# VectorE's order in the top-k zone of a two-layer decoder trunk, and one transfer moved in its second mixer

## The chip, the cores and the metric

One core of one Trainium2 chip (trn2). The metric is the device time of one execution in microseconds, the median of the runs. One more execution was recorded by the profiler; all rows below come from that one.

## What is computed

The reference is a decoder trunk of two layers over 256 tokens of width 1024, all in float32. Cut to what matters here:

```python
for l in range(2):
    h = x @ w_in[l] + b_in[l]                       # one projection, split into the groups' inputs
    y_lru = _rg_lru(...)                            # convolution, gates, linear recurrence
    y_nsa = _nsa(...)                               # attention: compressed, selected, window
    mix = concat([rms(y_lru), rms(y_nsa)]) @ w_out[l]
    x = layer_norm(ALPHA * x + mix)
    x = layer_norm(ALPHA * x + _peer(x, ...))

def _peer(x, wq, subkeys, u_tab, v_tab):            # 16384 experts, 8 heads, 16 chosen per head
    q = (x @ wq).reshape(T, 8, 2, 128)
    s = einsum('thcd,ckd->thck', q, subkeys)        # scores against 2 x 128 keys
    sv, si = top_k(s, 16)
    cv, ci = top_k(all 16 x 16 sums of the two halves, 16)
    experts, gate = ..., softmax(cv)
    act = gelu(x . u_tab[experts]);  y = (act * gate) . v_tab[experts]
```

The gates of the recurrence are two sigmoids of small block-diagonal matmuls (`lru_wa`, `lru_wx`).

## The kernel before, in words

One program runs everything on one core. A layer has two parts.

**The mixer.** Its steps (projections, convolution, recurrence, attention, output projection, norms) are named by short codes, and a string per layer, `ORDER[l]` (L29 to L38), sets the order in which they are issued; the loop that reads it is at L715. `d0` to `d5` are transfers of constants (`const_load`, L666), issued on SyncE's queue: `d0` the table `cmix`, `d1` the gate weights `lw` (512 KB, L670), `d2` and `d3` the halves of `cw1` (512 KB each, L672), `d4` `cw2` (L674), `d5` the residual in the first layer only. `V0` to `V3` are the convolutions on VectorE (L361, L364), `G0` to `G3` the gates of the recurrence, which read `xc` and `lw` on TensorE (L370); `g`, `c`, `q`, `k` are projections (`proj`, L322). In the second layer the buffers of the mixer are those that the stage before it used, so its constants can be loaded only when that stage's last matmuls have read them.

**The experts.** No gather is done: all 16384 experts' activations are computed densely, as 128 tiles of 128 experts (`u_tile`, L739). A tile is loaded (512 KB), split into a high and a low part, and multiplied in three passes. The split is `wtile` (L96): ScalarE casts the high part `hi` (L103), and POOL (for the first 14 tiles, `NPOOL`) or VectorE (for the rest) subtracts to get the low part `lo` (L104); TensorE then runs 24 matmuls (`col_mm`, L114), of which the third is the first to need `lo`. There are four buffers for the raw tile and three each for `hi` and `lo`. Queries 4 to 7 of the experts' heads are made by the same routine, two tiles each, split on VectorE (`query`, L768).

Beside the u-tiles runs the **top-k zone** (L750 to L920), list work on VectorE. `top(h)` (L791) takes the scores of head h (eight matmuls on TensorE, L798, a copy `ss` by ScalarE, L800) and finds the 16 best of 128 keys in four pieces, each a chain of five steps (`best16`, L784: maximum, index, replace, maximum, index). `pairs(g)` (L808) forms 50 candidate sums for eight lists (L812, L816) and finds their 16 best in eight pieces. `choices(g)` (L830) turns indices into experts by wide comparisons and sums (L834 to L874), and `turn_round` (L878) transposes the result on TensorE and copies it. `work()` (L892) strings these together as a generator; each piece yields what it is reckoned to cost on VectorE, and the loop at L914 keeps an account: a piece's cost is taken off `room`, and whenever `room` is negative the next u-tile is issued, which adds 2.88 (a POOL tile) or 1.66 (a VectorE tile). A query adds 2 x 2.88 and takes 2 x 1.22. By that account the program's order in the middle of the zone is: the last pieces of `pairs(0)`, both tiles of query 4, both of query 5, four pieces of `top(4)`, query 6, `top(5)`, u-tile 12, query 7, `top(6)`, u-tile 13, two pieces of `top(7)`, u-tile 14, one piece, u-tile 15, one piece, u-tile 16, then `pairs(1)`, `choices(0)`, `choices(1)`, with a u-tile after every 1.7 us or so of list work.

This is the order in which instructions are written down. A scheduler then orders each engine's instructions when the program is compiled; it may put an instruction of later in the program ahead of one that is not ready by its own reckoning. The next stage (L961) makes one-hot matrices and goes on with the u-tiles that are left, 124 in all before its end.

Of the kernel before, what the change touches and what calls it, by code (L numbers as in the profile page):

```python
# [20 lines left out]
D = 1024  # L21
S = 256
# [27 lines left out]
NPOOL = 14  # L50
# [27 lines left out]
def trunk_kernel(ctx: ExitStack, tc: tile.TileContext, x, xt, cst, lam, pvec, brow, w_in, w_lx, w_v, w_q4, lru_w,  # L78
# [13 lines left out]
    def bank():  # L92
        return psp.tile([128, 512], F32, tag="ps", name="ps")


    def wtile(src, shape, lo_eng, dst=None):  # L96
        n = int(np.prod(shape))
        raw = ring.tile([128, 1024], F32, tag="raw", name="raw", bufs=4)
        if dst is None:
            dst = (ring.tile([128, 1024], F32R, tag="hi", name="hi"), ring.tile([128, 1024], F32R, tag="lo", name="lo"))  # L100
        nc.sync.dma_start(raw[:, :n], src)
        hi, lo, raw = dst[0][:, :n], dst[1][:, :n], raw[:, :n]
        ACT.copy(hi, raw)  # L103
        lo_eng.tensor_tensor(lo, raw, hi, op=ALU.subtract)  # L104
        if len(shape) == 2:
            hi = hi.rearrange("p (a b) -> p a b", a=shape[0])
            lo = lo.rearrange("p (a b) -> p a b", a=shape[0])
        return hi, lo
# [5 lines left out]
    def col_mm(ps, w, xT, t=ALL):  # L114
        for c in range(NCH):
            mm3(ps, (w[0][:, c, :], w[1][:, c, :]), (xT[0][:, c, t], xT[1][:, c, t]), c == 0, c == NCH - 1)
# [149 lines left out]
    for l in range(NL):  # L266
# [461 lines left out]
        with tc.tile_pool(name="peer", bufs=1, reuse_waits="tile") as pp:  # L728
# [7 lines left out]
            def act_tile():  # L736
                return pp.tile([128, 2, S], F32, name="act", bufs=NACT)

            def u_tile(a):  # L739
                if a % 2 == 0:  # L740
                    ub[a] = bank()
                ps = ub[a - a % 2]
                col_mm(ps[:, HALF[a % 2]], wtile(u_tab[l, a], (8, 128), POOL if a < NPOOL else DVE), xT)
                if a % 2:
                    at = act_tile()
                    ACT.activation(at.rearrange("p a b -> p (a b)"), ps, AF.Gelu_apprx_tanh)  # L746
                    kept[a - 1] = spill.tile([128, 2, S], F32, name="kept%d" % (a - 1), bufs=1)
                    ACT.dma_start(kept[a - 1], at)

            with tc.tile_pool(name="topk", bufs=1, reuse_waits="tile") as tk:  # L750
# [17 lines left out]
                def query(h):  # L768
                    qh = tk.tile([128, 2, S], F32, name="qh", bufs=2)
                    if h < 2:  # L770
                        for tb in range(2):
                            ACT.copy(qh[:, :, TB[tb]], qT4[tb][:, 2 * h:2 * h + 2])
                    else:
                        ps = bank()
                        for c in range(2):
                            k = 2 * h + c - 4
                            if "w%d" % k in W:
                                raw_mm(ps[:, c * 256:c * 256 + 256], W["w%d" % k])
                            else:
                                col_mm(ps[:, c * 256:c * 256 + 256], wtile(wq[l, k], (8, 128), POOL if h < 4 else DVE), xT)  # L780
                        ACT.copy(qh.rearrange("p a b -> p (a b)"), ps)
                    qhs[h] = qh
# [8 lines left out]
                def top(h):  # L791

                    qh = qhs.pop(h)
                    ps = bank()
                    for tb in range(2):
                        for c in range(2):
                            k = tb * 2 + c
                            PE.matmul(ps[:, k * 128:k * 128 + 128], qh[:, c, TB[tb]], skt[:, c], start=True, stop=True)  # L798
                    ss = tk.tile([128, 4, 128], F32, name="ss", bufs=2)
                    ACT.copy(ss.rearrange("p a b -> p (a b)"), ps)  # L800
                    s2 = tk.tile([128, 4, 128], F32, name="s2", bufs=2)
                    for tb in range(2):
                        for c in range(2):
                            k, j = tb * 2 + c, tb * 4 + h % 4
                            best16(sv[:, h // 4, j, c], si[:, h // 4, j, c], ss[:, k], s2[:, k])
                            yield 1.45

                def pairs(g):  # L808

                    a, b = sv[:, g, :, 0], sv[:, g, :, 1]  # L810
                    for i in range(8):
                        DVE.tensor_tensor(cd[:, :, OFF[i]:OFF[i] + CNT[i]], a[:, :, i:i + 1].to_broadcast([128, 8, CNT[i]]),  # L812
                                          b[:, :, :CNT[i]], op=ALU.add)
                        if i % 4 == 3:
                            yield 1.2
                    DVE.tensor_tensor(cd[:, :, OFF[8]:NCAND], a[:, :, 8:16],  # L816
                                      b[:, :, 0:1].to_broadcast([128, 8, 8]), op=ALU.add)
                    for j in range(8):
                        best16(cv[:, g, j], ci[:, g, j], cd[:, j], c2[:, j])
                        yield 1.05  # L820
# [57 lines left out]
                def turn_round():  # L878
                    for w in range(3):
                        ps = bank()  # L880
                        for tb in range(2):
                            src = ev[:, w, tb] if w < 2 else gate[:, tb]
                            PE.transpose(ps[:, TB[tb]], src.rearrange("p g k -> p (g k)"), ident)
                        tok = ps[:, :256].rearrange("p (q i) -> p q i", i=2)
                        if w < 2:
                            DVE.tensor_copy(eT[:, :, w], tok)
                        else:
                            DVE.tensor_scalar(gT[:, :, 0], tok, GSC, None, op0=ALU.mult)
                            DVE.scalar_tensor_tensor(gT[:, :, 1], tok, GSC, gT[:, :, 0], op0=ALU.mult, op1=ALU.subtract)
                        yield 0.5  # L890

                def work():  # L892
                    for h in (2, 0, 1, 3):
                        yield from top(h)
                    yield from pairs(0)
                    query(4)
                    yield 2.44 - 5.76
                    for h in range(4, 8):
                        if h < 7:
                            query(h + 1)  # L900
                            yield 2.44 - 5.76
                        yield from top(h)
                    yield from pairs(1)
                    yield from choices(0)
                    yield from choices(1)
                    yield 1.0
                    yield from turn_round()
                    yield 4.0
# [3 lines left out]
                        q_rows(1)  # L912
                    query(h)
                a, room = 0, 0.0  # L914
                for cost in work():
                    room -= cost
                    while room < 0 and a < 96:
                        u_tile(a)
                        room += 2.88 if a < NPOOL else 1.66
                        a += 1  # L920

            with tc.tile_pool(name="dense", bufs=1, reuse_waits="tile") as dp:

# [356 lines left out]
```

## Time and profile before

| what | value |
|---|---|
| runs, median (lowest to highest) | 1939.76 us (1935.61 to 1939.79), 3 runs |
| the profiled execution, its own time | 1938.31 us |
| its span | 1936.5 us |
| busy: TensorE, VectorE, ScalarE, POOL | 98%, 69%, 50%, 4% |
| share of the chain that ended last: TensorE, VectorE, DMA | 88%, 8%, 2% |

Times are microseconds from the start of the span. A busy share is an average over the whole span; the top-k zones lie at about 160 to 300 us (first layer) and 1120 to 1270 us (second layer), the start of the second mixer at about 987 us. PEclk is the clock that TensorE was granted, as a share of 2.4 GHz. Matmuls are pipelined, so a tile's own time is best read from the chain of waits, where pieces don't overlap.

### The profile page before, as it was taken

Reading aid. Unit: us, or ns where it says so; the run is one execution under the profiler, and the core shown is the slowest. Engines: PE = TensorE matmul, PEld = TensorE weight load, DVE = VectorE, ACT = ScalarE, POOL = GpSimd, SP = SyncE. Lnnn points to the kernel's source line nnn. Section 1 sums busy time; section 2 is a strip of 40 time slices with the busy share of each in tenths; the row PEclk is TensorE's granted clock in tenths of the full one; section 3 lists DMA queues with packets and bytes.
Section 4 is the critical chain, followed back from the end, with each engine's and each line's share of the span. In section 5 each row is a group of like instructions: output and inputs, shape, how many; then the busy total and the mean of one; then the engine's idle time right before and its main releaser. Section 6 shows DMA issues by size and latency. Waiting matters only on the chain.

```text
span 1936.5 us, 32461 instructions
## 1 busy us (share of the span) xinstructions
PE 1894.0 (98%) x12580; PEld 1679.2 (87%) x12580; DVE 1330.6 (69%) x2553; ACT 966.3 (50%) x1579; POOL 83.1 (4%) x55
## 2 busy tenths in 40 slices
PE   8999899999999999999999998999999999999998
PEld 7858899999999888888777498999999998888886
DVE  5763994766666776767657549946666656777776
ACT  3635444555555555556445344444555555555553
POOL 0005200000000000000000062000000000000000
PEclk9999999999999999999999999999999999999999
DMA  7505557666667777888362054576666677778783
GB/s 267 175 1 172 153 191 236 211 207 192 204 203 242 244 241 240 282 283 300 140 227 66 0 187 154 189 236 212 196 203 201 201 245 240 244 243 286 250 265 106
DMA packets 130095, 393.91 MB, mean 203 GB/s; under 512 B 15634, under 2 KB 16404, under 8 KB 129812
## 3 DMA queue, kind: packets, MB, share of 16 engines
q1 hardware_dynamic: 111508, 358.28, 57.8%
q10 hardware_dynamic: 18432, 33.56, 4.7%
q8 instruction: 98, 1.61, 0.3%
q14 instruction: 57, 0.47, 0.1%
HBM read 357.18 MB, written 34.60 MB: 202 GB/s over the span
## 4 chain that ended last, share of the span: by engine, by line
PE 88%; DVE 8%; DMA 2%; issue 1%; ACT 1%; SPq 0%; POOL 0%; DVEq 0%; ACTq 0%; POOLq 0%
PE ps L112 39%; PE ps L995 34%; PE ps L954 3%; PE ps L119 3%; PE ps L590 3%; DVE lo L104 1%; PE ps L562 1%; DMA raw<-in_v_tab_dram 1%; PE ps L515 1%; DVE si L789 1%; DVE cd L812 1%; PE ps L232 1%; DVE s L787 1%; DVE si L786 0%; DVE t L866 0%
## 5 line engine op out<-in xcount | busy, mean ns | idle before, releaser
L104 DVE TENSOR_TENSOR lo<-raw,hi 128x1024 fp32r<-128x1024 f32 x516 | 635.1, 1232 | 396.4 <-ACT hi L103 396.0
L103 ACT CAST hi<-raw 128x1024 fp32r<-128x1024 f32 x548 | 575.1, 1050 | 663.4 <-PE ps L112 412.0
L112 PE MATMUL ps<-xThi,lo 128*128 128x256 f32 x2400 | 685.4, 286 | 20.0 <-DVE lo L104 19.7
L112 PE MATMUL ps<-xThi,hi 128*128 128x256 f32 x2400 | 693.5, 289 | 0.0
L112 PE MATMUL ps<-xTlo,hi 128*128 128x256 f32 x2400 | 684.0, 285 | 0.0
L995 PE MATMUL ps<-hi,W 128*128 128x512 f32 x1936 | 517.8, 389 | 0.0
L112 PEld LDWEIGHTS ps<-xThi,lo 128*128 128x128 f32 x2400 | 465.4, 194 | 21.9 <-DVE lo L104 21.2
L112 PEld LDWEIGHTS ps<-xThi,hi 128*128 128x128 f32 x2400 | 465.7, 194 | 0.9 <-issue 0.4
L112 PEld LDWEIGHTS ps<-xTlo,hi 128*128 128x128 f32 x2400 | 465.8, 194 | 0.3
L995 PEld LDWEIGHTS ps<-hi,W 128*128 128x128 f32 x1936 | 363.2, 188 | 75.4
L995 PE MATMUL ps<-lo,W 128*128 128x512 f32 x968 | 298.1, 389 | 0.2 <-DVE lo L104 0.2
L995 PEld LDWEIGHTS ps<-lo,W 128*128 128x128 f32 x968 | 181.6, 188 | 38.2 <-DVE lo L104 0.6
L986 ACT CAST W<-act 128x256 fp32r<-128x256 f32 x242 | 96.1, 402 | 94.6 <-PE ps L995 90.4
L987 DVE TENSOR_TENSOR W<-act,W 128x256 fp32r<-128x256 f32 x242 | 100.0, 422 | 9.5
L104 POOL TENSOR_TENSOR lo<-raw,hi 128x1024 fp32r<-128x1024 f32 x32 | 79.6, 2493 | 355.9 <-ACT hi L103 355.6
L972 DVE TENSOR_TENSOR act<-act,G 128x512 f32<-128x512 f32 x128 | 87.5, 685 | 6.6 <-DMA act<-kept 6.6
L958 ACT ACTIVATE G<-ps 128x256 f32<-128x256 f32 x256 | 81.2, 383 | 5.3
L943 DVE TENSOR_TENSOR ohg<-ohg,gT 128x2048 f16<-128x2048 f16 x64 | 78.2, 1225 | 2.0
L939 DVE TENSOR_TENSOR ohg<-iota,eT 128x2048 f16<-128x2048 f16 x64 | 77.9, 1220 | 0.0
L746 ACT ACTIVATE act<-ps 128x512 f32<-128x512 f32 x128 | 75.7, 591 | 0.1
L954 PE MATMUL ps<-ohg 128*128 128x128 f16 x1024 | 69.9, 219 | 0.0
L954 PEld LDWEIGHTS <-ohg 128*128 128x128 f16 x1024 | 58.8, 97 | 2.8
(256 smaller groups left out, 1179.6 us busy)
## 6 DMA issues: line engine op xcount, KB each, us to landing
raw<-in_u_tab_dram SPq DMA_DIRECT2D x256, 512.0 KB, 3.6
raw<-in_v_tab_dram SPq DMA_DIRECT2D x256, 512.0 KB, 4.2
kept<-act ACTq DMA_DIRECT2D x128, 256.0 KB, 2.5
act<-kept SPq DMA_DIRECT2D x128, 256.0 KB, 4.1
raw<-in_w_in_dram SPq DMA_DIRECT2D x24, 512.0 KB, 4.5
raw<-in_wq_dram SPq DMA_DIRECT2D x24, 512.0 KB, 3.6
ow<-in_w_out_dram SPq DMA_DIRECT2D x16, 512.0 KB, 7.8
qf<-in_w_q_dram SPq DMA_DIRECT2D x8, 512.0 KB, 3.8
```

The source lines that it names most:

```text
L103: ACT.copy(hi, raw)
L104: lo_eng.tensor_tensor(lo, raw, hi, op=ALU.subtract)
L112: PE.matmul(ps, a[m], b[n], start=start and i == 0, stop=stop and i == 2)
L746: ACT.activation(at.rearrange("p a b -> p (a b)"), ps, AF.Gelu_apprx_tanh)
L939: DVE.tensor_tensor(oh.rearrange("p q w a i -> p (q w) a i"), iota.unsqueeze(1).to_broadcast([128, 8, 128, 2]), eT[:, qs].rearrange("p q w ...
L943: DVE.tensor_tensor(og, oh[:, :, 0:1].to_broadcast([128, 4, 2, 128, 2]), gT[:, qs].unsqueeze(3).to_broadcast([128, 4, 2, 128, 2]), op=ALU. ...
L954: PE.matmul(ps[:, k * 128:k * 128 + 128], oh[:, q, 1, :, i], og[:, q, w, :, i], start=w == 0, stop=w == 1)
L958: ACT.activation(G[g][:, :, t1:t1 + 4], ps.rearrange("p (t g a) -> p g a t", g=2, a=64)[:, g], AF.Copy, scale=1.0 / GSC)
L972: i = DVE.tensor_tensor(act[a0], act[a0], G[a0 // 64][:, a0 % 64:a0 % 64 + 2, :], op=ALU.mult)
L986: ACT.copy(whi, at[:, a % 2])
L987: DVE.tensor_tensor(wlo, at[:, a % 2], whi, op=ALU.subtract)
L995: PE.matmul(accs[tb * 2 + hf], ww[m][:, TB[tb]], v[n][:, hf * 512:hf * 512 + 512], start=a == first[0] and (m, n) == (0, 0), stop=a == 127 ...
```

## The change

It has three edits. In the second layer's order, `d1` moves from behind `V3` to directly behind `d0`. The loop that issues the top-k zone stands in a block that keeps VectorE's instructions in the order in which they are written; the other engines are ordered as before. And a VectorE u-tile adds 1.6 to `room` instead of 1.66, so that 48 instead of 47 u-tiles are issued within the zone.

```diff
-         "c0 I1 I0 d0 d4 P c1 V0 d2 V2 V1 d3 V3 d1 G0 d5 G3 G1 T g1 b0 g0 b1 g2 h0 g3 G2 q2 h1 D S q3 q1 kv q0 "
+         "c0 I1 I0 d0 d1 d4 P c1 V0 d2 V2 V1 d3 V3 G0 d5 G3 G1 T g1 b0 g0 b1 g2 h0 g3 G2 q2 h1 D S q3 q1 kv q0 "
...
                 a, room = 0, 0.0
-                for cost in work():
-                    room -= cost
-                    while room < 0 and a < 96:
-                        u_tile(a)
-                        room += 2.88 if a < NPOOL else 1.66
-                        a += 1
+                with tc.manual_schedule(engines={mybir.EngineType.DVE}):
+                    for cost in work():
+                        room -= cost
+                        while room < 0 and a < 96:
+                            u_tile(a)
+                            room += 2.88 if a < NPOOL else 1.6
+                            a += 1
```

## Rows read from the trace of the kernel before

**Rows 1.** The page, busy time of each engine over the span.
```profile
PE 1894.0 (98%) x12580; PEld 1679.2 (87%) x12580; DVE 1330.6 (69%) x2553; ACT 966.3 (50%) x1579; POOL 83.1 (4%) x55
```
**Rows 2.** Busy time by stretch: stretch, length, busy us, PEclk, DMA share, GB/s.
```profile
205.00:215.00 10.00, 7.28 (x49) 7.07 (x49) 9.97 (x58) 5.35 (x7) 0.00 (x0) 0.83 0.33 109
231.00:245.00 14.00, 11.81 (x87) 11.61 (x86) 14.00 (x67) 4.64 (x7) 3.54 (x1) 0.88 0.33 114
256.00:266.00 10.00, 6.03 (x38) 5.82 (x38) 10.00 (x59) 1.47 (x2) 0.00 (x0) 0.83 0.47 165
...
1170.00:1180.00 10.00, 6.12 (x49) 5.71 (x48) 9.97 (x45) 4.97 (x6) 0.00 (x0) 1.00 0.31 91
1196.00:1208.00 12.00, 9.83 (x71) 9.63 (x70) 12.00 (x56) 2.70 (x3) 3.49 (x1) 0.86 0.39 133
1220.00:1235.00 15.00, 11.03 (x70) 10.82 (x69) 14.15 (x85) 3.63 (x4) 0.00 (x0) 0.77 0.60 191
```
**Rows 3.** Waits of TensorE, 155 to 300 and 1118 to 1286: us, times, longest.
```profile
PE ps L112 <- DVE lo L104: 8.9, 3, 4.0
...
PE ps L112 <- DVE lo L104: 10.0, 4, 4.0
```
**Rows 4.** Timeline of VectorE, 128-wide pieces: start us, duration us, instruction.
```profile
175.82 0.28 DVE L787 MATCH_REPLACE8 s<-sv,ss 128x128 f32<-128x128 f32 x1
176.14 0.30 DVE L788 MAX8 sv<-s 128x8 f32<-128x128 f32 x1
176.47 0.09 DVE L789 MATCH_VALUE_LOAD si<-sv,s 128x8 f32 x1
...
256.26 0.31 DVE L785 MAX8 sv<-ss 128x8 f32<-128x128 f32 x1
256.46 0.30 DVE L788 MAX8 sv<-s 128x8 f32<-128x128 f32 x1
...
257.43 0.31 DVE L785 MAX8 sv<-ss 128x8 f32<-128x128 f32 x1
```
**Rows 5.** Timeline of VectorE, additions, 50-wide pieces and splits.
```profile
200.30 2.88 DVE L812 TENSOR_TENSOR cd<-sv 128x128 f32<-128x128 f32 x6
...
206.27 0.20 DVE L785 MAX8 cv<-cd 128x8 f32<-128x50 f32 x1
...
207.06 0.21 DVE L785 MAX8 cv<-cd 128x8 f32<-128x50 f32 x1
...
209.42 1.22 DVE L104 TENSOR_TENSOR lo<-raw,hi 128x1024 fp32r<-128x1024 f32 x1
...
211.51 2.29 DVE L851 TENSOR_TENSOR ge<-cif,i 128x2048 f16<-128x2048 f16 x1
...
259.35 0.73 DVE L812 TENSOR_TENSOR cd<-sv 128x128 f32<-128x128 f32 x6
```
**Rows 6.** Timeline of ScalarE: copies of query 5 and of top4's scores.
```profile
224.52 0.58 ACT L781 COPY qh<-ps 128x512 f32<-128x512 f32 x1
225.00 0.59 ACT L800 COPY ss<-ps 128x512 f32<-128x512 f32 x1
```
**Rows 7.** TensorE: two tiles in the chain of waits; the matmuls of one top.
```profile
186.69 5.75 PE ps L112 x48
...
185.63 1.06 PE L798 MATMUL ps<-skt,qh 128*128 128x128 f32 x8
```
**Rows 8.** Timelines at the second mixer's start: SyncE's queue, VectorE, TensorE.
```profile
987.90 0.48 SPq L674 DMA_DIRECT2D cw<-in_cmp_w_dram  x1
...
990.39 0.54 SPq L670 DMA_DIRECT2D lw<-in_lru_w_dram  x1
...
995.27 0.48 DVE L364 SCALAR_TENSOR_TENSOR xc<-xpad,pvec_sb,xc 128x256 f32<-128x256 f32 x1
...
996.87 2.36 DVE L104 TENSOR_TENSOR lo<-raw,hi 128x1024 fp32r<-128x1024 f32 x2
...
997.39 2.83 PE L370 MATMUL ps<-xc,lw 128*128 128x256 f32 x12 [3.15 <-DMA lw<-in_lru_w_dram]
```

## The prediction

> **What bounds the kernel now.** I read the busy shares first: TensorE works 98% of the span [rows 1], so a change pays only where TensorE waits or runs at the lower of its two clock levels. Busy time cut into stretches shows where that is inside the top-k zones (155 to 300 us in the first layer, 1118 to 1286 us in the second): in six stretches [rows 2]. TensorE's idle time there is 2.72, 2.19 and 3.97 us in the first layer, 8.9 in all, and 3.88, 2.17 and 3.97 in the second, 10.0 in all. The granted clock falls in five of the six. Stretch times missing clock share gives 1.7 + 1.7 + 1.7 = 5.1 us in the first layer and 0 + 1.7 + 3.4 = 5.1 in the second: behind a short wait TensorE runs a while at 1.2 instead of 2.4 GHz. All that this zone can give back is thus 8.9 + 5.1 + 10.0 + 5.1 = 29 us. The list of waits names who ends them: VectorE's splits (`lo`, L104), and nothing else of any weight [rows 3]. VectorE is busy through nearly all six stretches, so each wait is a matter of order: list work stood in front of a split that TensorE wanted.
>
> VectorE's order now is not that of the program. `choices(0)` is written behind `pairs(1)`, yet its line L851 runs at 211.5 us, among the splits of queries 4 and 5 [rows 5]. And list instructions of two pieces are interleaved: the first maximum of one piece runs beside the second of the one before [rows 4].
>
> **The change, part by part.**
>
> *Program order, price of a piece.* `best16` is a chain: maximum, index, replace, maximum, index. Where neighbours are independent, a 128-wide maximum is followed after 0.20 us; where the next needs its result, after 0.33 (176.14 to 176.47), and behind a replace 0.32 (175.82 to 176.14) [rows 4]. A piece has three such joints. Interleaved, a 128-wide piece takes 1.17 us (256.26 to 257.43) and a 50-wide one 0.79 (206.27 to 207.06) [rows 4, 5]. In program order I add 3 x 0.125 = 0.37: 1.54 and 1.16. With three joints at 0.125 the lower bound is 0 (all hidden by a neighbour), the upper 0.4; I take nearly the upper, since program order puts the dependent ones side by side. The plan in `work()` reckons with 1.45 and 1.05, so it is some 0.1 us short per piece.
>
> [...]
>
> *Query 4's first split.* It stands behind all of `pairs(0)` in the program. The nine additions end at 203.18 us, held up now (2.88 us for six, 0.73 in the second group) [rows 5]; top(3)'s own joints, 4 x 0.37, lie partly in that hold. Eight pieces at 1.16 then end at 212.5. The split, now at 209.42 between two pieces, starts some 3.5 us later (3 to 4.6). The tiles before it are split on POOL and end where they do, so this wait grows from 2.7 to some 6.2, less what TensorE waits now for the query's second split, which will follow at once: 5.5. Bounds 2.7 and 6.7.
>
> *Queries 6 and 7, and u-tile 14.* The order in the program is Q4 Q5 top4 Q6 top5 u12 Q7 top6 u13, half of top7, u14, each Q being two tiles whose splits are VectorE's; u12 and u13 are split on POOL. Now VectorE fills the time with `choices(0)`; pinned, it cannot. It must wait for top4's scores, which TensorE computes behind Q5's tiles: the copy of query 5 is at 224.52, that of top4's scores at 225.00 [rows 6]. Only then come four pieces (4 x 1.54 = 6.2), then Q6's first split. A tile is 5.75 / 2 = 2.88 us on TensorE, the scores' matmuls about 0.8 to 1.06 [rows 7]. So:
> - before Q6: 0.7 (copy of the scores) + 6.2 + 1.2 (a split, [rows 5]) = 8.1 us without a split; TensorE has u12 (2.9) if it is put forward, and two matmuls (0.2): 5.0 idle.
> - before Q7: 1.1 (Q6's second split, overlapped) + 6.2 + 1.2 = 8.5, against two tiles and two matmuls, 6.0: 2.5 idle.
> - before u14: 1.1 + 6.2 + 3.1 + 1.2 = 11.6, against two tiles, u13, scores and two matmuls, 9.7: 1.9 idle.
>
> Bounds: nothing for each if the scores are computed early; and 7.9, 5.0 and 8.1 if TensorE, too, keeps strict program order, where each top's scores come behind the next query's tiles (0.7 + 6.2 + 1.2 - 0.2 without u12; the same less u12; the same with half of top7, 3.1, less u13). I take the sums above, because in the trace a ready instruction is put into a gap.
>
> *After u14.* A tile's share is 1.6 us of list plus 1.14 of split (two take 2.36, one 1.22 [rows 5, 8]), under 2.88: no wait, and the third stretch of each layer loses its reason. `room` 1.66 to 1.6 puts one more u-tile into the zone and one less into the next stage, whose number is the same in sum: 0. `turn_round` copies now wait in VectorE's queue for transposes that stand behind tiles on TensorE; a split behind them comes late by at least itself, 1.2, less two matmuls, 0.2: 1.0 once per layer. ACT's exponential and casts lie beside this work.
>
> *Clock.* Five falls cost 10.2 us, 2.0 each (1.7 to 3.4). For four or five waits per layer I take 3.5 falls: 7.1 instead of 5.1, 2.0 more per layer.
>
> Zone: waits 5.5 + 5.0 + 2.5 + 1.9 + 1.0 = 15.9. First layer 15.9 - 8.9 + 2.0 = +9.0, second 15.9 - 10.0 + 2.0 = +7.9.
>
> *Gate weights first (second mixer).* `d1` moves from the last to the second place of the five transfers on SyncE's queue, ahead of `d4`, `d2`, `d3`. TensorE waits 3.15 us for `lw`, until 997.39; its issue was at 990.39 and moves to about 987.9, where `d4` is now [rows 8], 2.5 us earlier, with about 1.1 MB less in front of it. The wait goes, but the next is near: the third convolution chain ends at 995.75, and the next projection's split, at 996.87, is done by 998.1, against 1000.2 now (997.39 + 2.83, where its work gets TensorE): 2.1 us gained, bounds 0 and 3.15. `d2` and `d3` come 0.5 MB later; they are needed later, at the first hidden layer, behind two more projections. The first mixer's order is unchanged.
>
> Sum: 9.0 + 7.9 - 2.1 = +14.8 on the profiled execution's 1938.3 us (its span is 1936.5, with 1.8 around it): 1953.1. That execution stands 1.5 us under the median of 1939.8, so I predict 1955 us; the cases below are set against the median too.
>
> **The rivals.**
> 1. *TensorE in strict program order too.* Waits 5.5 + 7.9 + 5.0 + 8.1 + 1.0 = 27.5, five falls, 10 us: 27.5 - 8.9 + 4.9 = +23.5 and 27.5 - 10.0 + 4.9 = +22.4, - 2.1: 1983 us. For it: rows 6, where the scores follow the next query's tiles. Against it: gaps are filled in this trace.
> 2. *Faster.* The scores of top(h) run on TensorE before the tiles of query h+1, so the four pieces lie beside those tiles, and u12 and u13 fill the rest. It is decided by whether top4's copy comes before Q5's. Left are the first wait (5.5) and one fall (2.4): 7.9 instead of 14.0 and 15.1, - 13.3 - 2.1: 1924 us; with no wait at all, 29 and 2.1 off, 1909.
> 3. *Order unchanged.* VectorE's order stays as it is, since the interleaving does not come from what is pinned: only the mixer counts, 1938.
> 4. *A piece costs no more in program order.* First wait 2.7, then 5.0 - 1.5, 2.5 - 1.5, 0, and 1.0: 8.2 a layer, clock as now: - 0.7 - 1.8 - 2.1: 1935. Rows 4 speak against it. [...]
>
> **How the numbers follow.** Forecast 0.44 (1945 to 1972), rival 1 0.13, rival 2 0.28, rivals 3 and 4 0.15 together. A measurement here tells 0.3%, 5.8 us, from no change: 1934 to 1945.6. Rivals 3 and 4 lie inside it. So faster 0.28, same 0.15, slower 0.57. The range must reach rival 2 and most of rival 1: 1918 to 1980; the forecast's own is 1945 to 1972.
>
> **What would show it.** Right: VectorE's L785 to L789 run piece by piece, a piece at 1.5 us; L851 for the first time behind the second group's pieces; TensorE waits before Q4, Q6, Q7 and u14, and not later; VectorE idle before L785 of top4, released by the copy of its scores. In the mixer L370 starts at about 994 and the next projection 2 us sooner. Wrong: TensorE's waits in the zones under 8.9 and 10.0 us, or the scores' copy of top4 ahead of query 5's.

## The result, and the profile after

The changed kernel takes 1970.03 us in the median of 4 runs (1969.45 to 1974.1). Against the kernel before the ratio is 1.0166 (95% interval 1.0147 to 1.0185): 30 us more by the medians, 32 by the ratio. The forecast was 15 us more, its range went to 1980. So the kernel is slower, as forecast, but by twice as much, and one step of the forecast's mechanism did not hold. The profiled execution is the longest of the four: 1974.1 us, span 1972.3.

The page says that TensorE has more idle time, not more work: its busy time grew by 8.6 us where the span grew by 35.8 [rows 1].

```profile
PE 1902.6 (96%) x12577; PEld 1686.3 (86%) x12580; DVE 1350.1 (68%) x2553; ACT 965.8 (49%) x1579; POOL 80.0 (4%) x55
```

The waits of TensorE, first layer from 155 to 345 us, then from 345 to 375, then the second layer from 1118 to 1345 (us, times, longest):

```profile
PE ps L112 <- DVE lo L104: 20.2, 3, 7.3
PE ps L798 <- ACT qh L781: 0.4, 1, 0.4
...
PE ps L112 <- DVE lo L104: 2.9, 1, 2.9
...
PE ps L112 <- DVE lo L104: 23.0, 4, 7.3
PE ps L798 <- ACT qh L781: 0.4, 1, 0.4
```

That is 23.5 us in the first layer and 23.4 in the second, against 8.9 and 10.0 [rows 3]. Three waits in a row are before query 4, query 6 and u-tile 14, the fourth is among `turn_round`'s copies. Busy time by stretch puts them there (stretch, length, busy us of TensorE, weight loads, VectorE, ScalarE, POOL, then the granted clock), to be read beside [rows 2]:

```profile
205.00:217.00 12.00, 5.78 (x44) 5.58 (x43) 11.15 (x69) 2.68 (x4) 0.00 (x0) 0.77 0.33 95
230.00:250.00 20.00, 13.01 (x85) 12.60 (x84) 16.21 (x68) 5.05 (x7) 2.36 (x1) 0.74 0.27 88
255.00:275.00 20.00, 12.68 (x91) 12.33 (x90) 15.85 (x72) 5.08 (x7) 0.00 (x0) 0.83 0.30 93
355.00:370.00 15.00, 12.13 (x90) 11.93 (x89) 9.52 (x12) 4.15 (x6) 0.00 (x0) 0.89 0.49 176
```

VectorE was full in [rows 2]; here it is busy 16 of 20 us in the second and third stretch. It waits too, and its timeline says for what (start, duration, instruction, idle time before it and what ended that):

```profile
175.11 0.28 DVE L785 MAX8 sv<-ss 128x8 f32<-128x128 f32 x1
176.68 0.28 DVE L785 MAX8 sv<-ss 128x8 f32<-128x128 f32 x1
...
206.40 0.20 DVE L785 MAX8 cv<-cd 128x8 f32<-128x50 f32 x1
207.56 0.19 DVE L785 MAX8 cv<-cd 128x8 f32<-128x50 f32 x1
...
214.54 3.48 DVE L104 TENSOR_TENSOR lo<-raw,hi 128x1024 fp32r<-128x1024 f32 x3
...
231.92 0.29 DVE L785 MAX8 sv<-ss 128x8 f32<-128x128 f32 x1 [8.94 <-ACT ss L800]
...
238.21 2.34 DVE L104 TENSOR_TENSOR lo<-raw,hi 128x1024 fp32r<-128x1024 f32 x2
...
258.33 0.29 DVE L785 MAX8 sv<-ss 128x8 f32<-128x128 f32 x1 [8.10 <-ACT ss L800]
...
267.76 1.21 DVE L104 TENSOR_TENSOR lo<-raw,hi 128x1024 fp32r<-128x1024 f32 x1
```

Pieces run one by one: a 128-wide piece takes 1.57 us (175.11 to 176.68) and a 50-wide one 1.16 [rows 4, 5: 1.17 and 0.79]. Twice VectorE stands idle for over 8 us until top 4's and top 6's scores are copied. Only then come the pieces (four before query 6, six before u-tile 14), and only behind them the split that TensorE wants. The timeline of ScalarE shows why the scores are late:

```profile
230.82 0.58 ACT L781 COPY qh<-ps 128x512 f32<-128x512 f32 x1
231.30 0.59 ACT L800 COPY ss<-ps 128x512 f32<-128x512 f32 x1
...
257.23 0.58 ACT L781 COPY qh<-ps 128x512 f32<-128x512 f32 x1
257.71 0.59 ACT L800 COPY ss<-ps 128x512 f32<-128x512 f32 x1
```

The copy of top 4's scores comes right behind that of query 5, top 6's right behind that of query 7, as in [rows 6]: TensorE computes them behind both tiles of the next query. In the kernel before that cost little, since VectorE did `choices(0)` meanwhile.

In the second mixer, SyncE's queue now issues `lw` ahead of `cw` and `cw1` [rows 8], and the wait for it (3.15 us) is gone:

```profile
1009.63 0.42 SPq L670 DMA_DIRECT2D lw<-in_lru_w_dram  x1
1010.40 0.48 SPq L674 DMA_DIRECT2D cw<-in_cmp_w_dram  x1
```

What TensorE still waits for from 985 to 1060 us is short:

```profile
PE ps L456 <- DVE h1r L454: 0.8, 1, 0.8
PE ps L370 <- DVE xc L364: 0.7, 1, 0.7
```

### The profile page after: what moved, and what is told of

It reads as the page before. It is cut to its first block, busy times and chain, and to the rows that moved or that the text cites. A ratio compares the mean times of both kernels' runs of the same rounds, so it can differ in the third digit from the quotient of the medians.

```text
span 1972.3 us, 32462 instructions
## 1 busy us (share of the span) xinstructions
PE 1902.6 (96%) x12577; PEld 1686.3 (86%) x12580; DVE 1350.1 (68%) x2553; ACT 965.8 (49%) x1579; POOL 80.0 (4%) x55
## 4 chain that ended last, share of the span: by engine, by line
PE 90%; DVE 5%; DMA 2%; ACT 1%; issue 1%; POOL 0%; SPq 0%; DVEq 0%; ACTq 0%; POOLq 0%
PE ps L112 42%; PE ps L996 34%; PE ps L955 3%; PE ps L590 3%; PE ps L119 3%; DMA raw<-in_v_tab_dram 1%; PE ps L562 1%; PE ps L515 1%; DVE lo L104 1%; PE ps L232 1%; DVE si L786 1%; DVE si L789 0%; PE ps L798 0%; DMA raw<-in_w_lx_dram 0%; DVE sv L788 0%
## 5 line engine op out<-in xcount | busy, mean ns | idle before, releaser
L785 DVE MAX8 sv<-ss 128x8 f32<-128x128 f32 x64 | 17.9, 280 | 78.0 <-ACT ss L800 77.7
```

## The experiments

Ratios are against the kernel before on the same chip (its medians there were 1938.8 to 1939.8 us). Where two versions ran on different chips, medians and ratios can differ by up to 3 us; both are then given. The runs with VectorE left free keep the 1.66 and the `turn_round` in the loop of the kernel before; the pinned ones, but for `e2_pin_only`, have 1.6.

### The two parts apart

`e1_d1_only` is the kernel before with the order string of the change; `e2_pin_only` has only the pinned block, with 1.66.

> The kernel before with only the gate weights moved (d1 behind d0 in the second layer). Theory (the mixer's stage from 1009 to 1060 us of after was 3.9 us shorter than before): 1936 us, 3 to 4 less than before, no half-clock interval near 1030 us. The prediction's own term was -2.1 (1937.7). Rival (the transfers behind d1 come late and take it back): 1940, no change.

Measured: 1935.03 us, ratio 0.9986 (0.9977 to 0.9995), 2.7 us less by the ratio, 3.8 by the medians. The transfer pays, about as forecast (2.1).

> The kernel after without the move of d1 and with room 1.66: VectorE pinned and nothing else. Theory (the pinned zone alone costs, 19 and 18 us in the two layers): 1974 us, +34 against before. Rival (1.6 in place of 1.66 has its part, because a tile more stands among the list work): 1965 or less.

Measured: 1975.94 us, ratio 1.0195 (1.0179 to 1.0210). The pinned zone is the whole loss: 37 us by the medians, 38 by the ratio. Less the 2.7 of `d1` that would be some 35, where the change lost 30 or 32; 1.6 in place of 1.66 may be worth the rest, but with intervals of 3 to 4 us to either side the two runs don't settle that.

### The late scores

```diff
-                def query(h):
+                def query(h, mid=None):
...
                         for c in range(2):
+                            if c and mid is not None:
+                                scores(mid)
...
-                            query(h + 1)
+                            query(h + 1, h)
```

`scores(h)` is the first half of `top(h)`: the eight matmuls and the copy. Pieces and splits keep their order.

> The kernel after, but the scores of top 4, 5 and 6 are issued between the two tiles of the next query in place of behind them; pieces and splits as in after. Theory (the waits before query 6 and u-tile 14 are the time in which VectorE waits for scores that stand behind a whole query): each of these two waits falls by about a tile, 2.9 us (6.6 to 3.8 and 7.3 to 4.4), with 0.5 to 1 us of clock per layer: 12 to 14 less than after, 1957 us. Rival (the waits come from the dearer pieces, whenever the scores arrive): waits as in after, 1970 us.

Measured: 1958.16 us, ratio 1.0105 (1.0089 to 1.0120), 12 us less than after. The waits from 155 to 345 us:

```profile
PE ps L112 <- DVE lo L104: 13.5, 3, 6.2
PE ps L800 <- ACT qh L783: 1.3, 1, 1.3
PE ps L112 <- POOL lo L104: 0.2, 1, 0.2
```

The one before query 4 is still 6.2; before query 6 there are 2.4 and 1.3 (for the query's copy), before u-tile 14 4.9. Moving eight matmuls by one tile took 5.7 us of waits out of each layer, with no piece made cheaper: the two waits fell from 14.3 to 8.6. That shows the place of the scores as a cause of them; what the other 8.6 us hang on this run does not show.

`e5_mid_free` makes the same edit with VectorE left free (and `d1` first).

> The kernel before with d1 moved and the scores of top 4 to 6 between the next query's tiles, VectorE's order left free. Theory (the late scores cost only because a pinned VectorE has to wait for them; left free it fills that time with choices(0)): as e1_d1_only, 1935 us, within 3. Rival (late scores cost TensorE time in any order): 1925 or less, since some 5 us per layer should go as they did in the pinned kernel (-12 for both).

Measured: 1931.21 us, ratio 0.9956 (0.9941 to 0.9970), 6 less than `e1_d1_only` by the ratios. Neither side was right: a free VectorE hides a good part of a late score, not all of it.

### The block ended ahead of `turn_round`

```diff
                     yield from choices(1)
                     yield 1.0
-                    yield from turn_round()
-                    yield 4.0
...
+                for cost in itertools.chain(turn_round(), (4.0,)):
+                    room -= cost
+                    while room < 0 and a < 96:
+                        u_tile(a)
+                        room += 2.88 if a < NPOOL else 1.6
+                        a += 1
```

> The kernel after, but the pinned block ends ahead of the turn_round step. Theory (TensorE's 2.9 us near 361 and 1341 us and the half-clock interval behind it, 1.7, come from splits that stand behind turn_round's copies): both go, 9 less than after, 1961 us. Rival (the wait is only moved to the next split, since the copies have to be made anyway): 1967 to 1970 us.

Measured: 1962.98 us, ratio 1.0121 (1.0106 to 1.0137), 7 us less than after by the medians, 9 by the ratios. Between 345 and 375 us TensorE no longer waits at all, and the granted clock no longer falls near there. In after, the timeline of VectorE shows what stood in the way:

```profile
360.07 0.76 DVE L886 CAST eT<-ps 128x256 f16<-128x256 f32 x2 [6.67 <-PE ps L883]
360.74 0.41 DVE L888 TENSOR_SCALAR gT<-ps 128x256 f16<-128x256 f32 x1
361.07 1.22 DVE L940 TENSOR_TENSOR ohg<-iota,eT 128x2048 f16<-128x2048 f16 x1
362.20 0.42 DVE L889 SCALAR_TENSOR_TENSOR gT<-ps,gT 128x256 f16<-128x256 f32 x1
362.54 3.49 DVE L104 TENSOR_TENSOR lo<-raw,hi 128x1024 fp32r<-128x1024 f32 x3
```

VectorE idles 6.67 us for the transposes with three splits queued behind the copies.

### The plan's prices alone

The kernel after, with a 128-wide piece at 1.57 in place of 1.45, a 50-wide one at 1.17 in place of 1.05, and the halves of the additions of `pairs` at 2.2 (first group) and 0.6 in place of 1.2. By this account u-tile 14, which VectorE splits, comes to stand between queries 6 and 7.

> The kernel after with the plan's prices set to the measured ones and nothing else; two more POOL tiles then stand ahead of query 4, and none between queries 6 and 7 or behind query 7. Theory (the wait before query 4 is the account running down by the pieces' joints and the held additions; the other waits are late scores, whose cover u12 and u13 were): the wait before query 4 falls from 6.2 to under 2, that before query 6 stays near 7, one before query 7 of 2 to 3 appears, and that behind query 7 stays at 7 to 8; sum per layer 17 to 20 against 23.5, time 1960 to 1968 us. Rival (the prices carry all the waits): 1945 or less.

Measured: 1962.05 us, ratio 1.0109 (1.0093 to 1.0125), 8 us less than after by the medians, 11 by the ratios. The waits of the first zone:

```profile
PE ps L112 <- DVE lo L104: 14.9, 4, 6.6
PE ps L798 <- ACT qh L781: 0.4, 1, 0.4
PE ps L112 <- POOL lo L104: 0.2, 1, 0.2
```

By place: 2.7 before query 4 (6.2 in after), 6.6 before query 6, unchanged, 0.3 before u-tile 14 and query 7, and 5.3 behind query 7, before u-tile 15. So the first wait is mostly the account's shortfall, and the wait before query 6 owes nothing to prices. The last wait fell, which I had not expected. VectorE's timeline shows why:

```profile
258.36 0.29 DVE L785 MAX8 sv<-ss 128x8 f32<-128x128 f32 x1 [8.18 <-ACT ss L800]
...
263.08 1.21 DVE L104 TENSOR_TENSOR lo<-raw,hi 128x1024 fp32r<-128x1024 f32 x1
```

It idles for top 6's scores as before, but three pieces stand between them and the split in place of six: 4.7 us in place of 9.4 (258.33 to 267.76 in after). TensorE has u-tile 13 (2.9 us) no more at that place, and 7.3 - 4.7 + 2.9 is 5.5.

### A written order that VectorE can follow

`e6_ahead_pin` is pinned, with `d1` first, `turn_round` outside, scores between the tiles, and each query one head earlier:

```diff
-                    for h in (2, 0, 1, 3):
-                        yield from top(h)
-                    yield from pairs(0)
-                    query(4)
...
+                    for h in (2, 0, 1):
+                        yield from top(h)
+                    query(4)
+                    yield 2.44 - 5.76
+                    yield from top(3)
+                    query(5, 4)
+                    yield 2.44 - 5.76
+                    yield from pairs(0)
+                    query(6, 5)
+                    yield 2.44 - 5.76
+                    yield from top(4)
+                    query(7, 6)
+                    yield 2.44 - 5.76
+                    for h in (5, 6, 7):
+                        yield from top(h)
```

> Pinned as in after (turn_round outside the block, d1 first), but each query is issued one head earlier: query 4 ahead of top 3, query 5 ahead of the first group's pairs, query 6 ahead of top 4, query 7 ahead of top 5, scores between the next query's tiles. Theory (pinning costs only by the waits that the order written down contains): VectorE has list work whenever scores are late, the waits before query 6 and u-tile 14 go, what stays is at most one of some 5 us per layer where the piece prices (1.45 and 1.05 against 1.57 and 1.17 measured) run the account down ahead of u-tile 14: 1920 to 1932 us, under before. Rival (a pinned VectorE is slower by its dearer pieces alone): 1945 or more.

Measured: 1937.63 us, ratio 0.9985 (0.9976 to 0.9994): a pinned kernel as fast as the one before, above what I expected. 9.2 us of waits stay per layer, 4.4 among the splits of queries 4 and 5 and 4.9 before the tiles behind query 7.

`e7_ahead_pin_cost` sets the measured prices in this order.

> As e6_ahead_pin, with the plan's prices set to the measured ones (128-wide piece 1.57, 50-wide 1.17, additions of the first group 2.2 per half, of the second 0.6). Theory (the rest of the waits is the account running down by 0.1 us and more per piece): waits in the zone under 3 us per layer, 1915 to 1925 us, below e6 by 3 to 10. Rival (prices are too small a matter to see): as e6 within 3.

Measured: 1928.40 us, ratio 0.9935 (0.9923 to 0.9948). The gain is as expected, the level is not: two waits of 3.0 us a layer stay. One is before query 4. For the other, VectorE's waits from 240 to 260 us give the reason, top 7's scores, written behind top 6's pieces:

```profile
DVE sv L787 <- ACT ss L802: 4.8, 1, 4.8
```

`e8_ahead_free` has the order of `e6_ahead_pin` with VectorE free.

> The kernel before with d1 moved and the queries a head earlier as in e6, VectorE's order free. Theory (a free VectorE already fills its time; its waits come from list work put ahead of a split, wherever the queries stand): 1930 to 1937 us, above e6. Rival (the written order is what counts, pinned or not): as e6 within 3.

Measured: 1931.92 us, ratio 0.9949 (0.9933 to 0.9965). It came where expected, but below `e6_ahead_pin`: with wrong prices a free order is the better one.

`e10_ahead_lead` changes `e7_ahead_pin_cost` in two places, and beats every other version:

```diff
-                    for h in (5, 6, 7):
-                        yield from top(h)
+                    yield from top(5)
+                    scores(7)
+                    yield from top(6)
+                    yield from top(7)
...
-                a, room = 0, 0.0
+                a, room = 0, -2.9
```

> As e7_ahead_pin_cost, with the account started at -2.9 (one u-tile more ahead of the first list work) and top 7's scores issued before top 6's pieces. Theory (its two waits of 3.0 per layer are query 4's split without a lead, and the 4.85 us in which VectorE waits for top 7's scores): waits in the zone under 1.5 per layer, no half-clock interval there, 1928 - 2 x (4.9 + 1.7) = 1915 us, 1910 to 1920. Rival (a later tile loses what is gained, since three buffers of parts cannot hold a longer lead): 1924 or more.

Measured: 1916.20 us, ratio 0.9879 (0.9864 to 0.9894), 23 us under the kernel before. The time came where expected, but a wait of 3.0 us is left where under 1.5 was expected, from 155 to 345 us:

```profile
PE ps L112 <- DVE lo L104: 3.0, 1, 3.0
```

It is the one before query 4, as long as in `e7_ahead_pin_cost`: the lead of a tile did not shorten it, VectorE only idled longer for scores ahead of the last eight pieces before it (6.27 us in place of 2.90). What went is the wait for top 7's scores. The two edits were not tried apart. In the busy times from 155 to 300 us TensorE has 141.86 of 145, and the granted clock is 0.99:

```profile
155.00:300.00 145.00, 141.86 (x1146) 140.38 (x1145) 110.72 (x451) 68.85 (x85) 38.14 (x16) 0.99 0.65 204
```

`e11_ahead_lead_free` has the same written order, not pinned.

> The same written order as e10_ahead_lead with VectorE left free (and turn_round where it was). Theory (free order puts list work ahead of splits at some 7 to 8 us of waits per layer whatever is written): 1925 to 1933 us, above e10 by 10 or more. Rival (the written order is all, pinned or free): within 4 of e10.

Measured: 1927.30 us, ratio 0.9934 (0.9921 to 0.9948), 11 above `e10_ahead_lead`; 7.2 and 7.4 us of waits in the two layers. So pinning is worth something, where the order and the prices are right; how much of the 11 us lies in the 1.66 and in `turn_round`'s place no run shows.

`e12_q4_pool` goes after the last wait: query 4's splits on POOL (`POOL if h < 5`).

> As e10_ahead_lead, with query 4's two splits on POOL in place of VectorE. Theory (the last wait, 3.0 us per layer before query 4, is its first VectorE split, 2.70 us in place of 1.21 since it stands beside a POOL split): the wait goes, with the half-clock stretch behind it: 1916 - 2 x (3.0 + 1.3) = 1907.5 us, 1904 to 1911. Rival (the account was short by a split anyway, so the wait moves to the next VectorE split, query 5's): 1914 or more.

Measured: 1922.12 us, ratio 0.9908 (0.9894 to 0.9922), 6 more than `e10_ahead_lead`. The rival has the time and the place: the wait comes back, 4.2 us long, before query 5's split, which stands behind top 3's pieces. Its reason, the account, is not what the trace shows. VectorE idles before the first of these pieces, for top 3's scores:

```profile
203.57 0.30 DVE L787 MAX8 sv<-ss 128x8 f32<-128x128 f32 x1 [5.88 <-ACT ss L802]
```

In `e10_ahead_lead` TensorE computed them at 193.91 us, ahead of query 4's tiles; with these tiles split on POOL they stand behind both, at 201.39. It is a late score once more.

## Why the prediction was wrong

Its terms per layer, and what the trace of after shows:

| step | forecast us | measured us |
|---|---|---|
| before query 4 | 5.5 | 6.2 |
| before query 6 | 5.0 | 6.6 + 0.4 |
| before query 7 | 2.5 | 0 |
| before u-tile 14 | 1.9 | 7.3 |
| `turn_round` | 1.0 | 2.9 |
| sum of waits | 15.9 | 23.5 and 23.4 |
| added beside the waits (clock) | 2.0 | 4.7 and 4.6 |
| `d1` first | -2.1 | -2.7 (`e1_d1_only`) |

The row on the clock is worked out. From the first matmul of the zone (L139) to the first of the one-hot matrices, the first layer took 202.4 us before (155.9 to 358.3) and 224.6 after (157.6 to 382.2). The u-tile that moved into the zone is 2.9 of the 22.2 between, and waits are 23.5 - 8.9 = 14.6: 4.7 are left, with the granted clock down in each of the four stretches above; the paragraph on the clock says how much of that it carries. The second layer goes alike (203.4 and 224.3, waits 13.4 more).

**Piece prices and the first wait: right.** 1.57 and 1.16 against 1.54 and 1.16. Query 4's split moved from 209.42 to 214.54, with its wait near the upper bound of 6.7. `e9_prices_only` confirms the cause: the account, told the true prices, gives 3.5 of the 6.2 back. (The ninth addition ends at 203.32 us, not 203.18, which changes nothing in the sum.)

**The failed step: "a ready instruction is put into a gap."** From it I took that u-tile 12 would stand in the gap before query 6 and that top 6's scores would not wait for query 7's tiles. In after, POOL had u-tile 12's low part at 233.41 us (231.05 + 2.36), in the middle of TensorE's wait, and TensorE didn't take it. Its timeline (start, duration) shows the tile's first two matmuls, which need no low part, ahead of the wait, and its third, which does, only behind the 46 that query 6 had left (the second of the pair at 247.68; the rows don't name tiles, but a tile's 24 matmuls repeat two on the high part and one on the low, and two low ones in a row stand only at such a change of tile):

```profile
232.37 0.36 PE L112 MATMUL ps<-xThi,hi 128*128 128x256 f32 x1
232.57 0.28 PE L112 MATMUL ps<-xTlo,hi 128*128 128x256 f32 x1
239.47 0.58 PE L112 MATMUL ps<-xThi,lo 128*128 128x256 f32 x1 [6.62 <-DVE lo L104]
239.85 0.41 PE L112 MATMUL ps<-xThi,hi 128*128 128x256 f32 x1
240.06 0.41 PE L112 MATMUL ps<-xTlo,hi 128*128 128x256 f32 x1
...
247.44 0.28 PE L112 MATMUL ps<-xThi,hi 128*128 128x256 f32 x1
247.56 0.28 PE L112 MATMUL ps<-xTlo,hi 128*128 128x256 f32 x1
247.68 0.40 PE L112 MATMUL ps<-xThi,lo 128*128 128x256 f32 x2
```

The chain of waits has query 6's tiles, u-tile 12 and query 7 without a break up to the scores:

```profile
238.21 1.22 DVE lo L104
239.47 16.89 PE ps L112 x116
256.36 0.89 PE ps L798 x8
```

So nothing but the order held u-tile 12 back. The order was fixed when the program was compiled; that the scheduler then reckoned POOL's low part later than query 6's is likely, but not shown. Hence 7.0 where I had 5.0; for this wait rival 1's 7.9 was the closer sum. `e9_prices_only` agrees: there u-tile 12 stands ahead of query 4, and the wait before query 6 is 6.6 all the same. For u-tile 14, its 8.1 against 7.3 measured; the forecast's 1.9 let top 6's pieces begin behind query 7's second split, as if their scores ran ahead of query 7's tiles, while VectorE in fact waited 8.10 us for them. Only top 5's scores did go into a gap (they are copied at 232.65), and u-tile 12 then stood ahead of query 7: no wait there. By the sum of waits (23.5) the truth lay between the forecast's 15.9 and rival 1's 27.5, and nearer the rival. Rival 2 named what the zone lacked; the written order did not bring it, and `e3_scores_mid` brought part of it.

**`turn_round`.** I counted the late split with one tile's work. In the trace three splits stand behind the copies, and VectorE idles 6.67 us first: 2.9 in place of 1.0.

**Clock.** I took 3.5 falls a layer, and there were four. The greater error is in what I set against them: missing clock times stretch also counts the idle time inside a stretch, and makes the kernel before lose 5.1 us a layer. The starts of the matmuls tell it better: at 1.2 GHz one follows another after 0.21 us (239.85 to 240.06 above), at 2.4 GHz after 0.12 (247.44 to 247.56). By a count of those stretches 44 and 42 matmuls ran at 1.2 GHz in the two layers of the kernel before, and 84 and 80 in after. A slow one costs 0.09 us more, so that is 4.0 us a layer before and 7.7 in after: 3.7 of the 4.7 and 4.6 us in the table, the rest is open. A longer wait did not always bring a longer stretch: behind 6.6 us 27 matmuls ran at 1.2 GHz, behind 7.3 us 17.

**Rival 4**, a piece that costs no more in program order: the trace speaks against it, 1.57 in program order against 1.17 interleaved. An operation that needs nothing from the one before does start sooner here (0.20 us against 0.33 [rows 4]).

**The mixer: right.** `d2` and `d3` coming later cost nothing that shows.

## What to carry to other kernels

Pinning an engine to program order turns the places where the program waits on another engine into idle time: before doing so, write the order such that each input is asked for one step ahead, and see behind what the producer of that input stands in its own engine's queue. An account that plans such an order needs prices measured in that order (some 0.1 us a piece and 1 us for each half of the first group's additions cost 8 to 11 us in all here). And do not count on a ready instruction to fill a gap on its engine: u-tile 12 did not, because it stood behind query 6 in TensorE's order.

## What the runs showed of the hardware that was not expected

A VectorE split beside one on POOL is held. In `e10_ahead_lead` query 4's two splits start at 195.64 us, while POOL splits a tile from 194.91 to 197.25 (columns: count, shortest, median and longest in ns, first and last start):

```profile
L104 DVE TENSOR_TENSOR lo<-raw,hi x2: 1211/1954/2697, 195.6 to 198.3; 128x1024 fp32r<-128x1024 f32 x2
L104 POOL TENSOR_TENSOR lo<-raw,hi x1: 2342/2342/2342, 194.9 to 194.9; 128x1024 fp32r<-128x1024 f32 x1
```

The first takes 2.70 us, the second, alone, 1.21. The list pieces, with one tensor as input, keep their 1.57 beside POOL (maxima at 186.22 and 187.79 us of the same trace, a POOL split from 185.39 to 187.78). The Trainium skill, "SBUF — State Buffer", section "SBUF: two separate sides", calls the port pair of the two engines an exclusive lock, which an operation of VectorE with two inputs in SBUF also takes part in, against one of POOL that reads SBUF; the trace agrees, the held split ending 1.09 us behind POOL's. The 1.5 us by which it is held are half of the wait before query 4 there; `e12_q4_pool` took the hold away and lost more by a late score.

The granted clock need not fall behind the same wait. From 205 to 215 us the first layer of `e1_d1_only` has the instructions of the kernel before and the same 2.7 us wait before query 4, but the clock stays at 1.00 where it was 0.83, as it did in the second layer of the kernel before [rows 2]:

```profile
205.00:215.00 10.00, 6.12 (x49) 5.71 (x49) 9.97 (x56) 5.75 (x7) 0.00 (x0) 1.00 0.31 103
```

A term for the clock that rests on one profiled execution is good to a fall or two, some 2 to 4 us at the prediction's 2.0 us a fall.
